# A transformer layer on one core: the second branch's projection moves from the merge into the attention

## The chip, the cores and the metric

The kernel runs on one core of a Trainium2 chip. The metric is the time of one execution in microseconds (us); a smaller one is better. Below, PE is the matrix engine (TensorE), DVE the vector engine, ACT the scalar engine, POOL the GpSimd engine, and SP the engine that here only issues transfers. Line numbers (L206) are those of the kernel's file.

## The reference

One layer of a diffusion backbone works on 256 latent tokens and 256 context tokens, 2048 wide. Cut to what matters here:

```
m_lat = split(silu(c) @ w_ada + b_ada, 6)       # modulation: six rows of 2048, the same for context
h  = rms_norm(x) * (1 + m_lat[1]) + m_lat[0]
p  = h @ w_in                                    # keys, values, queries and gates of both branches
oa = attention(rope(norm(qa)), ka_all, va_all)   # 16 heads of 128, 4 key heads
ob = diff_attention(rope(norm(qb)), kb_all, vb_all)   # 8 heads, two softmaxes subtracted, then a norm
merged = sigmoid(ga) * (oa @ w_br_a) + sigmoid(gb) * (ob @ w_br_b)
x1 = x + m_lat[2] * (merged @ w_out)
x2 = x1 + m_lat[5] * swiglu(rms_norm(x1) * (1 + m_lat[4]) + m_lat[3])
```

Here w_br_a is 2048x2048 and w_br_b 1024x2048. Only the latent tokens are carried on; context tokens give keys and values.

## The kernel before

Every large product is computed in three passes: an operand is split into a high part and the remainder (low part), and high x high (L210), high x low (L211) and low x high (L212) are summed in PSUM by `mm3`. Tokens stand in two tiles of 128 (`tk` 0 and 1). Weights come in pieces of 256 rows by 512 columns, 512 KB. `load_w` (L196) takes a piece by a transfer on SP's queue into a ring of 7 buffers (`wraw`), makes the high part on ACT (`whi`, L205) and the low part on DVE (`wlo`, L206), three buffers each. A piece is then 12 matmuls of 128x512 on PE: two row blocks, two token tiles, three passes. `project` (L534) is a generator: it loads pieces ahead, yields after each, and calls `tick()` (deferred work) and the function given as `side`. A result column group (`cg`) is 512 columns wide; its sums are handed to `evac`.

The stages around the change are these. After the context and the first half of the input projection come the attention's 32 units, 16 of branch b (the differential one) and 16 of branch a. A unit is cut into `front` (scores `s`, maximum on DVE L578, exponential on ACT L581) and `back` (transposes `ptp` L646, copies `pT` by ACT and DVE, product `o`). Between units the `filler` (L703) runs projection pieces so that PE has work while a softmax is under way: the query groups, whose evacuation is a long chain of norm and rotation (`norm_rope`, L393 to L416), and the eight gate projections, whose results ACT copies (L685) and POOL writes to DRAM (`gate_d`, L686). At unit 8 stands the keys stage: the keys of branch b's second half, then those and the values of branch a, with norms as well.

Two things run beside the filler's pieces, called by `side_work` (L692). `later` is the modulation: pieces of w_ada (`ada_pieces`, L353), each a 512 KB transfer and DVE instructions of 128x1024 that add a scaled row block to an accumulator (L364); its chunks 2, 4 and 3 are spread over the middle of the kernel, 96 such instructions. `chores` are the chains of the keys. Before, each call takes a chore, and every second call an ada as well.

The merge (from L736) goes over four column groups. For each, `load_gates` reads the stored gates of branch b back (POOL, L767) and takes their sigmoid (ACT, L768); w_br_b is projected in 4 pieces and its result multiplied by the gate (DVE, L775); then the same for w_br_a in 8 pieces, multiplied and added (L777, L778), and `turn` transposes the sum for the output projection. At the start the attention's results are split into high and low parts by `o_parts` (L216), and the last units' work is finished among the first pieces.

The order of the instructions on each engine is fixed when the program is built, by a list scheduler that follows the order of the code and priorities; `issue_after(x)` binds an instruction behind another. An engine works its list in that order, and an instruction that waits holds those behind it. The buffers that a transfer waits for are the ring's.

Of the kernel before, what the change touches and what calls it, by code (L numbers as in the profile page):

```python
# [11 lines left out]
F32 = mybir.dt.float32  # L12
# [23 lines left out]
WK = 2  # L36
# [10 lines left out]
def hybrid_block(ctx: ExitStack, tc: tile.TileContext, t: dict, out: bass.AP):  # L47
# [143 lines left out]
        nc.vector.tensor_scalar(out=neglam, in0=neglam, scalar1=-LAM_INIT, scalar2=None, op0=ALU.add)  # L191


    last_lo = []

    def load_w(src, r0, c0, nk=WK, in_big=False):  # L196
        raw = wp.tile([P, WK, CG], F32, tag="wraw", bufs=WRAW, name="wraw")
        nc.sync.dma_start(out=raw[:, 0:nk], in_=src[r0:r0 + nk * P, c0:c0 + CG].rearrange("(k p) c -> p k c", p=P))
        if in_big:
            both = big_tile("wbig", F32R).rearrange("p (h k c) -> p h k c", h=2, c=CG)  # L200
            hi, lo = both[:, 0], both[:, 1]
        else:
            hi = wp.tile([P, WK, CG], F32R, tag="whi", bufs=WHI, name="whi")
            lo = wp.tile([P, WK, CG], F32R, tag="wlo", bufs=WLO, name="wlo")
        nc.scalar.copy(out=hi[:, 0:nk], in_=raw[:, 0:nk])  # L205
# [472 lines left out]


    gate_d = dram.tile([2, 2, P, D], F32, name="gate_d")  # L680

    def gate_evac(w, cg):
        def f(tk, ps):
            g = scratch("gate")
            nc.scalar.copy(out=g, in_=ps)  # L685
            nc.gpsimd.dma_start(out=gate_d[w, tk, :, cg * CG:(cg + 1) * CG], in_=g)  # L686
        return f

    turns = [0]
    chores = [later_keys]  # L690
# [8 lines left out]
    gates = [(w, cg) for w in range(2) for cg in range(4)]  # L699
    units = [("b", u) for u in range(16)] + [("a", u) for u in range(16)]  # L700
    done, ready, started = set(), set(), []

    def filler():  # L703

        while len(started) < len(q_order) or gates:
            may = not gates or len(started) < 2 or a_done
            if may and len(started) < len(q_order) and len(started) - len(done) < 2:
                q = q_order[len(started)]
                started.append(q)
                for _ in q_group(*q):  # L710
                    pieces[0] += 1
                    yield None
                after(7, lambda q=q: ready.add(q))
            else:
                w, cg = gates.pop(0)
                for _ in project(w_in, xT, NKT, (GA0, GB0)[w] + cg * CG, gate_evac(w, cg), side=side_work):
                    pieces[0] += 1
                    yield None

    pieces = [0]  # L720
    all_pieces = (len(q_order) + len(gates)) * (NKT // WK)
    fill = filler()
    work = []

# [33 lines left out]
    w_bra, w_brb, w_out = t["w_br_a"][0], t["w_br_b"][0], t["w_out"][0]  # L758
    mT = Parts("mT", NKT)
    for cg in range(4):  # L760
        m = [scratch(f"m{tk}") for tk in range(2)]
        gs = {}

        def load_gates(w):
            for tk in range(2):
                g = scratch("gin", tag="p", bufs=4)
                nc.gpsimd.dma_start(out=g, in_=gate_d[w, tk, :, cg * CG:(cg + 1) * CG])  # L767
                nc.scalar.activation(out=g, in_=g, func=AF.Sigmoid)  # L768
                gs[w, tk] = g

        def gated(w):
            def f(tk, ps):
                g = gs[w, tk]
                if w == 1:
                    nc.vector.tensor_tensor(out=m[tk], in0=ps, in1=g, op=ALU.mult)  # L775
                else:
                    nc.vector.tensor_tensor(out=g, in0=ps, in1=g, op=ALU.mult)  # L777
                    nc.vector.tensor_tensor(out=m[tk], in0=m[tk], in1=g, op=ALU.add)  # L778
                    after(2 + tk, turn(tk))
            return f  # L780

        def turn(tk, cg=cg, m=m):
            def f():
# [4 lines left out]
                split(hi, lo, tp.rearrange("p (h q) -> p h q", h=4))  # L788
            return f

        if cg == 0:
            o_parts(4)
            o_parts(5)
        load_gates(1)
        for k, _ in enumerate(project(w_brb, oT, BH, cg * CG, gated(1), kt0=AH)):
            take(later, k % 2)
            if cg == 0:
                for w in list(work):
                    if next(w, w) is w:
                        work.remove(w)  # L800
                if k > 0:
                    o_parts(k - 1)
        if cg == 0:
            assert not work
            o_parts(3)
        load_gates(0)
        for k, _ in enumerate(project(w_bra, oT, AH, cg * CG, gated(0))):
            take(later, k % 2)
# [151 lines left out]
```

## Time and profile before

| | us |
|---|---|
| median of three runs | 1750.39 |
| lowest, highest | 1748.45, 1753.29 |
| profiled execution | 1752.44 |
| its span on the core | 1750.7 |
| PE busy in it | 1709.3 (98%) |
| DVE busy | 1128.9 (64%) |
| ACT busy | 773.2 (44%) |

The mean granted clock of PE in this execution is 0.993 of full speed. The profile counts as busy the time in which an engine has an instruction under way; matmuls overlap, so that one lasts 0.39 us while they follow each other every 0.22. Times in the trace count from the start of the span. In it, the keys stage lies at about 475 to 575, the passage from branch b to a at about 575 to 625, the units of a end at about 785, and the merge lasts to about 1000. The value PEclk of a window is the mean granted clock there; 1.00 is 2.4 GHz and 0.50 is 1.2 GHz.

### The profile page before, as it was taken

The page shows a single profiled execution, that of the slowest core. Times are in us where ns is not written, and L with a number is a line of the kernel's source. Part 1 is how long each engine was busy: PE and PEld are TensorE (multiplying, and loading weights), DVE is VectorE, ACT ScalarE, POOL GpSimd, SP SyncE. Part 2 cuts the span into 40 slices and gives each one's busy share as a digit, 9 for nine tenths or more (in the row PEclk, how much of TensorE's full clock was granted, in tenths as well). Part 3 has the DMA queues.
Part 4 walks back from the last instruction along what each step waited for, and adds up shares of the span by engine and source line. Part 5 has one row for each costly group of instructions (what it writes and reads, how often), then busy time and mean ns, then how long its engine had stood idle before and what let it go on. Part 6 is the DMA issues. An engine that isn't in the chain of part 4 may idle for free.

```text
span 1750.7 us, 21655 instructions
## 1 busy us (share of the span) xinstructions
PE 1709.3 (98%) x8106; PEld 1378.3 (79%) x8106; DVE 1128.9 (64%) x1416; ACT 773.2 (44%) x1061; POOL 126.5 (7%) x188
## 2 busy tenths in 40 slices
PE   5999999999999999999999999999999999999998
PEld 3767778887877788878888878888888888888887
DVE  4754658888798786968556664555566555454554
ACT  4422223246655566575444454444444444333332
POOL 2100001001132200001000100000000000000000
PEclk8999999999999999999999999999999999999999
DMA  9867785687776665648786756677777777666662
GB/s 271 281 222 262 239 306 181 195 269 246 223 231 222 204 236 175 212 133 278 245 288 225 251 176 190 203 239 233 238 239 239 234 237 232 208 197 214 219 204 90
DMA packets 190600, 393.47 MB, mean 225 GB/s; under 512 B 13120, under 2 KB 25488, under 8 KB 189984
## 3 DMA queue, kind: packets, MB, share of 16 engines
q1 hardware_dynamic: 183824, 369.71, 65.2%
q0 software_dynamic: 6672, 22.39, 4.1%
q8 instruction: 63, 1.03, 0.2%
q14 instruction: 41, 0.34, 0.1%
HBM read 383.62 MB, written 8.42 MB: 224 GB/s over the span
## 4 chain that ended last, share of the span: by engine, by line
PE 88%; DVE 5%; issue 3%; DMA 2%; ACT 1%; POOL 1%; SPq 1%; ACTq 0%; DVEq 0%; POOLq 0%
PE mm L211 27%; PE mm L210 26%; PE mm L212 26%; PE ada L266 2%; DVE wlo L206 1%; DMA wraw<-in_w_in_dram 1%; PE ptp L646 1%; PE s L626 1%; PE o L664 1%; ACT whi L205 1%; PE ftp L902 1%; DVE ada L364 0%; PE o L211 0%; DMA wada<-in_w_ada_dram 0%; PE o L210 0%
## 5 line engine op out<-in xcount | busy, mean ns | idle before, releaser
L206 DVE TENSOR_TENSOR wlo<-wraw,whi 128x1024 fp32r<-128x1024 f32 (+1 forms) x506 | 611.0, 1210 | 472.0 <-ACT whi L205 471.6
L205 ACT CAST whi<-wraw 128x1024 fp32r<-128x1024 f32 (+1 forms) x506 | 527.2, 1043 | 800.1 <-PE mm L212 685.4
L211 PE MATMUL mm<-wlo,hT 128*128 128x512 f32 x696 | 271.0, 389 | 2.0 <-DVE rstd L129 2.0
L210 PE MATMUL mm<-whi,hT 128*128 128x512 f32 x696 | 272.8, 392 | 0.0
L212 PE MATMUL mm<-whi,hT 128*128 128x512 f32 x696 | 271.2, 390 | 0.1
L210 PE MATMUL mm<-whi,xT 128*128 128x512 f32 x640 | 257.8, 407 | 2.3 <-ACT xT L215 1.8
L211 PE MATMUL mm<-wlo,xT 128*128 128x512 f32 x640 | 254.7, 398 | 4.9 <-DVE wlo L206 4.9
L212 PE MATMUL mm<-whi,xT 128*128 128x512 f32 x640 | 252.9, 395 | 0.0
L211 PEld LDWEIGHTS mm<-wlo,hT 128*128 128x128 f32 x696 | 130.7, 188 | 28.8 <-DVE wlo L206 2.4
L212 PEld LDWEIGHTS mm<-whi,hT 128*128 128x128 f32 x696 | 130.6, 188 | 27.7 <-DVE hT L216 0.5
L210 PEld LDWEIGHTS mm<-whi,xT 128*128 128x128 f32 x640 | 121.5, 190 | 39.3 <-issue 9.3
L364 DVE SCALAR_TENSOR_TENSOR ada<-wada,sc,ada 128x1024 f32<-128x1024 f32 x120 | 152.1, 1278 | 0.0
L210 PEld LDWEIGHTS mm<-whi,hT 128*128 128x128 f32 x696 | 130.7, 188 | 26.5
L211 PEld LDWEIGHTS mm<-wlo,xT 128*128 128x128 f32 x640 | 122.2, 191 | 30.5 <-DVE wlo L206 6.4
L212 PEld LDWEIGHTS mm<-whi,xT 128*128 128x128 f32 x640 | 122.0, 191 | 25.6
L210 PE MATMUL mm<-whi,fT 128*128 128x512 f32 x352 | 137.2, 390 | 0.0
L212 PE MATMUL mm<-whi,fT 128*128 128x512 f32 x352 | 137.0, 389 | 0.0
L211 PE MATMUL mm<-wlo,fT 128*128 128x512 f32 x352 | 136.9, 389 | 0.0
L210 PEld LDWEIGHTS mm<-whi,fT 128*128 128x128 f32 x352 | 66.1, 188 | 14.6 <-issue 0.8
L211 PEld LDWEIGHTS mm<-wlo,fT 128*128 128x128 f32 x352 | 66.1, 188 | 13.7
L212 PEld LDWEIGHTS mm<-whi,fT 128*128 128x128 f32 x352 | 66.1, 188 | 13.6
L210 PE MATMUL mm<-whi,cT 128*128 128x512 f32 x192 | 75.9, 395 | 0.4 <-ACT cT L215 0.4
(226 smaller groups left out, 2089.5 us busy)
## 6 DMA issues: line engine op xcount, KB each, us to landing
wada<-in_w_ada_dram SPq DMA_DIRECT2D x192, 512.0 KB, 4.5
wraw<-in_w_in_dram SPq DMA_DIRECT2D x154, 512.0 KB, 4.7
wraw<-in_w_ff_gate_dram SPq DMA_DIRECT2D x88, 512.0 KB, 4.2
wraw<-in_w_ff_up_dram SPq DMA_DIRECT2D x88, 512.0 KB, 4.1
wraw<-in_w_ff_down_dram SPq DMA_DIRECT2D x88, 512.0 KB, 4.8
wraw<-in_w_br_a_dram SPq DMA_DIRECT2D x32, 512.0 KB, 4.9
wraw<-in_w_out_dram SPq DMA_DIRECT2D x32, 512.0 KB, 5.2
wraw<-in_w_br_b_dram SPq DMA_DIRECT2D x16, 512.0 KB, 5.7
```

The source lines that it names most:

```text
L205: nc.scalar.copy(out=hi[:, 0:nk], in_=raw[:, 0:nk])
L206: last_lo.append(nc.vector.tensor_tensor(out=lo[:, 0:nk], in0=raw[:, 0:nk], in1=hi[:, 0:nk].bitcast(F32), op=ALU.subtract))
L210: nc.tensor.matmul(ps, lhsT=ah, rhs=wh, start=first, stop=False)
L211: nc.tensor.matmul(ps, lhsT=ah, rhs=wl, start=False, stop=False)
L212: nc.tensor.matmul(ps, lhsT=al, rhs=wh, start=False, stop=last)
L266: nc.tensor.matmul(aps[32 * g:32 * g + 32, 0:ncol], lhsT=cst[:, k, :], rhs=rhs, start=(k < 4), stop=(k >= NKT - 4))
L364: nc.vector.scalar_tensor_tensor(out=dst, in0=wt, scalar=sc[:, 0, kt:kt + 1], in1=dst, op0=ALU.mult, op1=ALU.add)
L626: nc.tensor.matmul(sps[i], lhsT=qT[rows, x, hh, tk * P:(tk + 1) * P], rhs=kT["b", grp][y][rows, hh, :], start=(n == 0), stop=(n == 2))
L646: nc.tensor.transpose(out=tp[:, kt * P:(kt + 1) * P], in_=p[:, kt * P:(kt + 1) * P], identity=ident)
L664: nc.tensor.matmul(op[:, 0:BV], lhsT=pT[:, kt, :], rhs=vb[:, kt, hh * BV:(hh + 1) * BV], start=(kt == 0), stop=(kt == 3))
L902: nc.tensor.transpose(out=tp[:, j * P:(j + 1) * P], in_=act[tk][:, j * P:(j + 1) * P], identity=ident)
```

## The change

The four column groups of w_br_b become the last entries of the filler's list, behind the eight gates: 16 pieces more between the units (128 instead of 112). As with the gates, ACT copies the sums and POOL writes them to DRAM, into a new tensor `prod_d`; one function, `to_dram`, serves both. The splits of branch b's output (`o_parts` 4 and 5) come just before, and those of branch a's first three quarters after units a6, a10 and a14.

`side_work` takes a chore first, and an ada only when there was no chore left and the keys stage of branch b is not running (`quiet`); then every second time, or two times of three once branch a has begun. The 96 ada of the chunks 2, 4 and 3 lay so before: 51 ahead of the keys stage, 9 in it, 28 among the a units and 8 in the merge. Now it is 53 ahead, none in the keys stage and 43 until the merge.

The merge keeps only w_br_a. `load_gated` is a generator of six steps for a column group, one per piece: reading a product back (L779), reading a gate (L783), its sigmoid (L786, bound behind the latest `whi`), and for branch b the product on DVE (L789, bound behind the latest `wlo`); then the gate of branch a.

```
-    def side_work():
-        turns[0] += 1
-        if turns[0] % 2:
-            take(later, 1)
-        take(chores[-1], 1)
+        if next(chores[-1], chores[-1]) is chores[-1] and not quiet:
+            turns[0] += 1
+            take(later, 1 if turns[0] % (3 if a_done else 2) else 0)
...
+    others += [(prod_d, oT, AH, t["w_br_b"][0], 0, cg) for cg in range(4)]
...
+                if kt0 and cg == 0:
+                    for g in (4, 5):
+                        o_parts(g)
+                for _ in project(w, src, BH if kt0 else NKT, c0 + cg * CG, to_dram(dst, cg), kt0=kt0, side=side_work):
...
+            quiet.append(True)
             for _ in keys("b", 1):
                 on()
                 take(fill, 2)
+            quiet.clear()
...
-    drain(fill)
+        if br == "a" and u % 4 == 2 and u > 4:
+            o_parts(u // 4 - 1)
+    for _ in fill:
+        on()
...
+        def load_gated():
             for tk in range(2):
+                m.append(scratch(f"m{tk}"))
+                nc.gpsimd.dma_start(out=m[tk], in_=prod_d[tk, :, cg * CG:(cg + 1) * CG])
+                yield None
+                for w in (1, 0):
+                    g = scratch("gin", tag="p", bufs=4)
+                    nc.gpsimd.dma_start(out=g, in_=gate_d[w, tk, :, cg * CG:(cg + 1) * CG])
+                    yield None
+                    with tc.issue_after(last_hi[-1].ins):
+                        nc.scalar.activation(out=g, in_=g, func=AF.Sigmoid)
+                    if w == 1:
+                        with tc.issue_after(last_lo[-1].ins):
+                            nc.vector.tensor_tensor(out=m[tk], in0=m[tk], in1=g, op=ALU.mult)
+                gs.append(g)
...
-        if cg == 0:
-            o_parts(4)
-            o_parts(5)
-        load_gates(1)
-        for k, _ in enumerate(project(w_brb, oT, BH, cg * CG, gated(1), kt0=AH)):
-            take(later, k % 2)
...
+        gates = load_gated()
+        for k, _ in enumerate(project(w_bra, oT, AH, cg * CG, gated)):
+            if k > 3:
+                take(later, 1)
+            if cg == 0 and k < 4:
+                on()
+                if k == 3:
+                    assert not work
+                    o_parts(3)
+            take(gates, 1)
```

How the order on the engines moves is shown at three places. The first is DVE in the keys stage of branch b; before, it reads (wlo is a weight's low part, nr, sq, ss and rstd belong to a norm of keys, kbT1 are keys turned, ada4 an accumulator of the modulation):

```order
L364 SCALAR_TENSOR_TENSOR ada4_2851<-wada2_4175,sc_107,ada4_2851 128x1024
L416 TENSOR_TENSOR nr_4184<-nr_4184,rstd_4181 128x512
L216 TENSOR_TENSOR kbT1_4040<-ktp_4190,kbT1_4039 128x4x128
L401 TENSOR_REDUCE ss_4238<-sq_4236 128x8
L410 TENSOR_TENSOR nr_4243<-kb1_118,rp_kb_1707 128x512
L129 TENSOR_SCALAR rstd_4240<-ss_4238 128x8
L412 TENSOR_TENSOR sq_4236<-kb1_118,rp_kb_1707 128x512
L206 TENSOR_TENSOR wlo_4262<-wraw_4259,whi_4261 128x1024
L414 TENSOR_TENSOR nr_4243<-nr_4243,sq_4236 128x8x32
L415 TENSOR_TENSOR nr_4243<-nr_4243,sq_4236 128x8x32
L206 TENSOR_TENSOR wlo_4280<-wraw_4277,whi_4279 128x1024
```

After the change the corresponding stretch, the norms of the same keys, reads:

```order
L206 TENSOR_TENSOR wlo_4317<-wraw_4314,whi_4316 128x1024
L416 TENSOR_TENSOR nr_4281<-nr_4281,rstd_4278 128x512
L216 TENSOR_TENSOR kbT1_4145<-ktp_4287,kbT1_4144 128x4x128
L129 TENSOR_SCALAR rstd_4336<-ss_4334 128x8
L410 TENSOR_TENSOR nr_4339<-kb1_118,rp_kb_1707 128x512
L412 TENSOR_TENSOR sq_4332<-kb1_118,rp_kb_1707 128x512
L206 TENSOR_TENSOR wlo_4358<-wraw_4355,whi_4357 128x1024
L414 TENSOR_TENSOR nr_4339<-nr_4339,sq_4332 128x8x32
L415 TENSOR_TENSOR nr_4339<-nr_4339,sq_4332 128x8x32
L206 TENSOR_TENSOR wlo_4376<-wraw_4373,whi_4375 128x1024
L416 TENSOR_TENSOR nr_4339<-nr_4339,rstd_4336 128x512
```

The row of ada4 (L364), which stood ahead of the end of a norm (L416) there and eight times more in the stage, is gone; the rows of wlo and of the norms alternate alone.

The second place is PE at the end of branch a's units. Before, the transposes of a unit's probabilities (ptp, four each) and the product that uses them (o from pT) stand one behind the other:

```order
L646 MATMUL ptp_7015<-ident_75,p_6947 128x128 x4
L646 MATMUL ptp_7022<-ident_75,p_6958 128x128 x4
L210 MATMUL o_7029<-pT_7014,vah_4611 128x256
L211 MATMUL o_7029<-pT_7014,vah_4611 128x256
L212 MATMUL o_7029<-pT_7014,val_4612 128x256
```

After, pieces of w_br_b (mm from oT4 and oT5, 12 matmuls each, of which one row stands here) lie between them:

```order
L646 MATMUL ptp_7312<-ident_75,p_7194 128x128 x4
L646 MATMUL ptp_7319<-ident_75,p_7205 128x128 x4
L210 MATMUL mm_7249<-whi_7328,oT4_6721 128x512
...
L210 MATMUL mm_7249<-whi_7349,oT5_6724 128x512
...
L210 MATMUL o_7365<-pT_7311,vah_4692 128x256
L211 MATMUL o_7365<-pT_7311,vah_4692 128x256
```

So two pieces come between the transposes and their product, where there was nothing.

The third place is POOL's list where the merge begins. Before, only reads of gates (gin, L767) stood there, of tensors written long ago. After, it reads (gate is here the copy of a product; adac_sb belongs to the modulation):

```order
L687 DMA prod_d_2817<-gate_7243 128x512
L687 DMA prod_d_2817<-gate_7246 128x512
L783 DMA gin_7485<-gate_d_2816 128x512
L783 DMA gin_7507<-gate_d_2816 128x512
L687 DMA prod_d_2817<-gate_7397 128x512
L372 DMA adac_sb_7404<-in_b_ada_dram 32x512
L687 DMA prod_d_2817<-gate_7400 128x512
L372 DMA adac_sb_7404<-in_b_ada_dram 32x512 x3
L779 DMA m0_7451<-prod_d_2817 128x512
L779 DMA m1_7531<-prod_d_2817 128x512
```

Two of the gates are read ahead of the last two writes of products; the first read of a product (m0) stands behind the last two writes and the biases.

One more place in words: on DVE the splits of oT4 and oT5 stood in the merge before. Now that of oT4, which the first piece of w_br_b needs, stands behind the norm of the last query group of branch a, ahead of that norm's last three rows; PE has there, between the group's last piece and that first one, the product of a unit and a unit's scores.

## Rows read from the trace of the kernel before

**Rows 1.** The page, part 1: engine, busy us, share of the span, instructions.

```profile
PE 1709.3 (98%) x8106; PEld 1378.3 (79%) x8106; DVE 1128.9 (64%) x1416; ACT 773.2 (44%) x1061; POOL 126.5 (7%) x188
```

**Rows 2.** Windows: from:to, length, busy us of each engine, PEclk, DMA share, GB/s.

```profile
475.00:550.00 75.00, 71.23 (x329) 55.31 (x328) 67.18 (x108) 42.83 (x73) 24.93 (x17) 0.95 0.69 217
...
575.00:625.00 50.00, 46.71 (x223) 37.67 (x222) 38.48 (x58) 22.28 (x40) 5.96 (x9) 0.97 0.68 218
625.00:750.00 125.00, 125.00 (x667) 106.55 (x666) 105.95 (x160) 82.47 (x146) 7.76 (x9) 1.00 0.59 200
750.00:800.00 50.00, 46.45 (x247) 38.36 (x246) 34.37 (x51) 38.13 (x69) 4.36 (x8) 0.97 0.40 127
800.00:1000.00 200.00, 199.96 (x900) 164.37 (x899) 125.78 (x130) 90.92 (x105) 18.19 (x34) 1.00 0.79 265
...
1025.00:1725.00 700.00, 700.00 (x3135) 578.79 (x3134) 379.00 (x343) 290.46 (x298) 8.60 (x16) 1.00 0.70 220
```

**Rows 3.** Windows, finer, around two of the stretches at the lower clock.

```profile
497.10:500.52 3.42, 3.42 (x9) 2.68 (x9) 1.89 (x4) 0.63 (x1) 2.72 (x1) 0.50 0.74 187
...
780.42:783.84 3.42, 3.42 (x14) 3.23 (x15) 2.30 (x2) 3.39 (x5) 0.00 (x0) 0.50 0.30 97
```

**Rows 4.** Waits of PE, 470 to 620, then 755 to 800: total us, times, longest.

```profile
PE mm L211 <- DVE wlo L206: 4.4, 3, 2.3
PE ptp L646 <- ACT junk_o L667: 1.3, 1, 1.3
PE s L626 <- ACT p L581: 1.2, 3, 0.7
...
PE o L210 <- DVE pT L216: 2.3, 2, 1.3
```

**Rows 5.** Lines of DVE, 486 to 548: instructions, busy us, mean ns, idle before.

```profile
L206 DVE TENSOR_TENSOR wlo<-wraw,whi 128x1024 fp32r<-128x1024 f32 x16 | 19.4, 1219 | 0.0
L364 DVE SCALAR_TENSOR_TENSOR ada<-wada,sc,ada 128x1024 f32<-128x1024 f32 x8 | 10.2, 1276 | 0.0
```

**Rows 6.** Timeline of PE, 492 to 498: start, length, then [idle before <-releaser].

```profile
496.58 0.50 PE L211 MATMUL mm<-wlo,xT 128*128 128x512 f32 x1 [2.29 <-DVE wlo L206]
```

**Rows 7.** Timeline of PE, 606 to 609.5, and of DVE, 598 to 612.

```profile
608.94 0.50 PE L211 MATMUL mm<-wlo,xT 128*128 128x512 f32 x1 [1.96 <-DVE wlo L206]
...
602.68 0.68 DVE L401 TENSOR_REDUCE ss<-sq 128x4 f32<-128x512 f32 x1
...
607.67 1.22 DVE L206 TENSOR_TENSOR wlo<-wraw,whi 128x1024 fp32r<-128x1024 f32 x1
```

**Rows 8.** Timeline of DVE, 695 to 708, and of PE, 702 to 708.

```profile
700.50 0.69 DVE L401 TENSOR_REDUCE ss<-sq 128x4 f32<-128x512 f32 x1 [1.14 <-ACT sq L399]
...
705.50 1.21 DVE L206 TENSOR_TENSOR wlo<-wraw,whi 128x1024 fp32r<-128x1024 f32 x1
...
706.93 0.39 PE L211 MATMUL mm<-wlo,xT 128*128 128x512 f32 x1
```

**Rows 9.** Timeline of PE, 776 to 783.

```profile
776.66 0.28 PE L211 MATMUL o<-pT,vah 128*128 128x256 f32 x1
776.78 0.29 PE L212 MATMUL o<-pT,val 128*128 128x256 f32 x1
...
779.76 0.36 PE L210 MATMUL o<-pT,vah 128*128 128x256 f32 x1 [1.26 <-DVE pT L216]
```

**Rows 10.** Lines of ACT, 800 to 1000.

```profile
L768 ACT ACTIVATE gin<-gin 128x512 f32<-128x512 f32 x12 | 7.6, 633 | 16.7 <-DMA gin<-gate_d 13.2 <-DVE ada L364 3.4
```

**Rows 11.** Source L686, then L767: issues of GpSimd (ns), and landing of their DMAs.

```profile
L686 POOL DMA_DIRECT2D gate_d<-gate x16: 539/584/633, 420.6 to 765.3; - x16
...
DMA to landing us min/median/max: 2.6/4.5/7.2
...
DMA to landing us min/median/max: 3.2/4.6/6.8
```

**Rows 12.** Windows: 612 to 796 as a whole.

```profile
612.00:796.00 184.00, 180.55 (x955) 152.72 (x954) 146.85 (x216) 124.87 (x219) 11.05 (x15) 0.99 0.56 189
```

More of the change, by code (lines that the diff above doesn't have):

```diff
@@ L204, in load_w @@
             lo = wp.tile([P, WK, CG], F32R, tag="wlo", bufs=WLO, name="wlo")
-        nc.scalar.copy(out=hi[:, 0:nk], in_=raw[:, 0:nk])
+        last_hi.append(nc.scalar.copy(out=hi[:, 0:nk], in_=raw[:, 0:nk]))
         last_lo.append(nc.vector.tensor_tensor(out=lo[:, 0:nk], in0=raw[:, 0:nk], in1=hi[:, 0:nk].bitcast(F32), op=ALU.subtract))
@@ L680, in hybrid_block, with to_dram @@
     gate_d = dram.tile([2, 2, P, D], F32, name="gate_d")
-    def gate_evac(w, cg):
+    prod_d = dram.tile([2, P, D], F32, name="prod_d")
+    def to_dram(dst, cg):
         def f(tk, ps):
@@ L685, in f @@
             nc.scalar.copy(out=g, in_=ps)
-            nc.gpsimd.dma_start(out=gate_d[w, tk, :, cg * CG:(cg + 1) * CG], in_=g)
+            nc.gpsimd.dma_start(out=dst[tk, :, cg * CG:(cg + 1) * CG], in_=g)
         return f
     turns = [0]
+    quiet = []
     chores = [later_keys]
     def side_work():
-        turns[0] += 1
-        if turns[0] % 2:
-            take(later, 1)
-        take(chores[-1], 1)
+        if next(chores[-1], chores[-1]) is chores[-1] and not quiet:
+            turns[0] += 1
+            take(later, 1 if turns[0] % (3 if a_done else 2) else 0)
     q_order = [("b", g) for g in range(2)] + [("a", g) for g in range(4)]
-    gates = [(w, cg) for w in range(2) for cg in range(4)]
+    others = [(gate_d[w], xT, 0, w_in, (GA0, GB0)[w], cg) for w in range(2) for cg in range(4)]
+    n_gates = len(others)
+    others += [(prod_d, oT, AH, t["w_br_b"][0], 0, cg) for cg in range(4)]
     units = [("b", u) for u in range(16)] + [("a", u) for u in range(16)]
@@ L703, in filler @@
     def filler():
-        while len(started) < len(q_order) or gates:
-            may = not gates or len(started) < 2 or a_done
+        while len(started) < len(q_order) or others:
+            may = not others or len(started) < 2 or a_done
             if may and len(started) < len(q_order) and len(started) - len(done) < 2:
@@ L754, in hybrid_block, with gated @@
         work.append(back(br, u, pr))
-    drain(fill)
-    w_bra, w_brb, w_out = t["w_br_a"][0], t["w_br_b"][0], t["w_out"][0]
+        if br == "a" and u % 4 == 2 and u > 4:
+            o_parts(u // 4 - 1)
+    for _ in fill:
+        on()
+    w_bra, w_out = t["w_br_a"][0], t["w_out"][0]
     mT = Parts("mT", NKT)
     for cg in range(4):
-        m = [scratch(f"m{tk}") for tk in range(2)]
-        gs = {}
-        def load_gates(w):
+        m, gs = [], []
+        def load_gated():
             for tk in range(2):
[L766 to L780, printed above, removed]
+                m.append(scratch(f"m{tk}"))
[11 more added lines that the diff above has]
+                gs.append(g)
+        def gated(tk, ps):
+            g = gs[tk]
+            nc.vector.tensor_tensor(out=g, in0=ps, in1=g, op=ALU.mult)
+            nc.vector.tensor_tensor(out=m[tk], in0=m[tk], in1=g, op=ALU.add)
+            after(2 + tk, turn(tk))
         def turn(tk, cg=cg, m=m):
@@ L789, in turn @@
             return f
-        if cg == 0:
-            o_parts(4)
-            o_parts(5)
-        load_gates(1)
-        for k, _ in enumerate(project(w_brb, oT, BH, cg * CG, gated(1), kt0=AH)):
-            take(later, k % 2)
[L797 to L808, printed above, removed]
+        gates = load_gated()
[8 more added lines that the diff above has]
+            take(gates, 1)
     drain(later)
```

7 lines of the change are left out of this document (3 added, 4 removed).

## The prediction

> **What bounds the kernel now.** I began with the engine line of the page. TensorE (PE) is busy 1709.3 of 1750.7 us, 98%; the vector engine (DVE) 64%, the scalar engine (ACT) 44% [rows 1]. PE's own work is the bound, and the order listing shows that the change leaves it alone: 7145 PE rows before, 7149 after. So only time that PE loses can be won: time in which it stands still, and time at the lower clock.
>
> Then I cut the part that the change touches into windows [rows 2]. From 625 to 750 us (first units of the softmax branch a), from 800 to 1000 (merge) and from 1025 to 1725 PE has no idle time to speak of, at a granted clock of 1.00. Three windows lose time: 475 to 550 us (71.23 busy of 75, clock 0.95), 575 to 625 (46.71 of 50, 0.97), 750 to 800 (46.45 of 50, 0.97). Standing still: 3.77 + 3.29 + 3.55 = 10.6 us. The clock: (1 - 0.95) x 75 + 0.03 x 50 + 0.03 x 50 = 6.75 us. In finer windows this is four stretches of 3.42 us at 0.50, the lower level (1.2 of 2.4 GHz), two of them in the first window (the first and the last of the four in [rows 3]); half of 4 x 3.42 is 6.8, the same sum. PE stood shortly before each of them, so a stall costs its length and then 1.7 us. All told 10.6 + 6.75 = 17.4 us. That is the ceiling of the gain.
>
> Third, the waits of these windows [rows 4]: matrix multiplications that wait for a weight's low part (wlo) on DVE, 4.4 us in three waits; scores and transposes that wait for ACT, 2.5; at the end of the attention the second product (o) for the transposed probabilities' low part (pT), 2.3.
>
> **The change part by part.** A matmul of 128x512 takes 700.00 / 3135 = 0.223 us [rows 2], so a piece of a projection (12) takes PE 2.7 us. On DVE it takes one wlo, 1.22, and a modulation piece (ada) another 1.28 [rows 5].
>
> (1) Keys stage, 475 to 550. PE stands 2.29 us for a wlo [rows 6]. In this stage DVE has 67.18 of 75 us of work [rows 2], in bursts, because the norms of the keys come on top of wlo and ada; in the listing nine ada lie in it, as in the piece shown with the change. Afterwards there are none: 9 x 1.28 = 11.5 us of DVE work leave, far more than the 3.77 that PE stood. The scores' waits for ACT I put to the same root, since the maximum that ACT needs first is made on DVE (L578), in the same queue. What is late next is a wlo behind a norm alone. I keep 1 us of loss; gain 3.77 + 3.75 - 1 = 6.5.
>
> (2) Passage from branch b to a, 575 to 625. The burst of the q norm, from the first sum (602.68) to the end of the wlo behind it (607.67 + 1.22), takes 6.2 us of DVE, and PE stood 1.96 us at 608.94 [rows 7]. The same burst at 700.50 to 706.71 cost nothing, PE going on at 706.93 [rows 8], since DVE came to it earlier. With chores ahead of ada the burst meets a shorter queue, but the chain is the same: I keep 1 us. Gain 3.29 + 1.5 - 1 = 3.8.
>
> (3) End of the attention, 750 to 800. Before, the last units stand nearly bare: transposes and the product that uses them follow one another (the fence of the change), and PE stood 1.26 us at 779.76 for pT, then fell to half clock [rows 9]. The change brings 16 more pieces of filler (43 us of PE work, taken out of a merge that was full), two of them, 5.4 us, between a unit's transposes and its product. That covers the wait. Gain 3.55 + 1.5 = 5.05.
>
> (4) A new hand-over. The filler's first piece with oT4 comes after the last q group. PE has from that group's end 12 matmuls of 0.12 us (776.66 to 776.78 in [rows 9]), 6 of 0.223 and 8 more until the first that needs the low part of oT4: about 4.6 us. DVE does the norm of q first, 5.0 us from the first sum to what stands behind it [rows 8], begun some 0.5 us before the group's end, since half of its results is complete 1.3 us ahead and ACT squares it in between; then the split of oT4, 128x1024 as a wlo, 1.2 us: ready at 5.7 us. So 1.1 us of stall; if an ada and a wlo ahead of it are still running it is 1.28 + 1.22 more, 3.6, and then 1.7 for the clock, 5.3. If DVE is ahead, as at 700, it is 0. I take 1.1, the nearer to [rows 8].
>
> (5) Round trip of the products. ACT copies each of the 8 results (0.63, by ACT's sigmoid of 128x512 [rows 10]), GpSimd (POOL) writes it to DRAM and reads it back. The reads stand in POOL's queue behind the last write's landing; ACT's sigmoids and DVE's new product L789 stand in front of casts and wlo. For the first group: the first half of the last product leaves PE 1.3 us before T0 (the end of that piece); + 0.63 copy + 0.58 issue + 4.5 landing = T0 + 4.4; read 0.58 + 4.6 = T0 + 9.6 [rows 11]. By the order PE has 10.7 us of pieces, one unit's product and eight transposes, and wants the wlo behind L789 at T0 + 13.9; less 1.22 and 0.7 L789 must start by T0 + 12.0. Slack 2.4. With the slowest landings of the rows, 7.2 and 6.8, it misses by 2.5, and costs 4.2 with the clock. In the three later groups a read issued 2.0 us after the group before ended is followed by the sigmoid and a cast that PE wants 11.7 us after; slack about 2.3. I take 0, for the median landings; the range holds 4.2. A gain is excluded, since PE loses nothing there today.
>
> (6) DVE among the a units. Its work there was 146.85 of 184 us [rows 12], and now has 16 wlo more, some 15 ada that came from the keys and the merge, and 5 splits fewer: 146.85 + 19.5 + 19.2 - 6.1 = 179 plus what the filler brings on the half units, at most 192, over 184 + 43 - 8 = 219 us. That is 82 to 88%. The window 625 to 750 had 85% without a loss [rows 2], so nothing is charged, at 0 to 4 bursts like the one at 606. The weights' DMA: two ada loads for three pieces are 5 x 0.52 MB in 3 x 2.7 + unit work, some 11.5 us, 228 GB/s; the merge ran at 265 [rows 2]. Nothing.
>
> (7) Merge: out go w_br_b's pieces and 8 ada. It was at 199.96 of 200, so this saves nothing there.
>
> Sum: 6.5 + 3.8 + 5.05 - 1.1 = 14.3 us. The profiled execution took 1752.44, so 1738.1; from the median of the runs, 1750.39, 1736.1. I give 1737.
>
> A rule that speaks against (5): by the Trainium skill, page "SBUF — State Buffer", section "A bandwidth-pool intuition that's wrong (but worth ruling out)", a transfer that GpSimd issues and that takes about 620 ns alone takes about 3100 ns under a DVE copy, as its descriptors cannot be written. The trace does not show it: with DVE 85% busy the gate writes issue in 539 to 633 ns and land in 2.6 to 7.2 us [rows 11]. Nothing in the sum rests on it; were it so for the new products, the first rival below would be its form.
>
> **The rivals.**
>
> Slower: the round trip holds the weights. Its place is L789 and the sigmoids in front of wlo and cast in the merge, which today loses nothing. For it: the chain write, landing, read is new, and today's writes have their landing hidden by hundreds of us. Against: the median landings leave 2.3 us. Price: if landings were doubled (9.0 and 9.2), the first group would be 9.1 - 2.4 = 6.7 late + 1.7 clock, the three later ones 4.6 - 2.3 + 1.7 = 4.0 each: 20.4 against the gain of 14.3, that is 6 us slower, about 1757. It begins beyond a landing of 6.9 us and decides at about 8.5.
>
> Smaller: the hand-over (4) costs its upper end, 5.3, and the keys keep half of their stall (2.3 more): 14.3 - 4.2 - 2.3 = 7.8, 1743. For it: DVE is denser there than at 700. Against: the splits of oT0 to oT2 come between the units.
>
> Same: DVE is the hidden bound of the denser a units, and each of the four a bursts stalls as that at 606 did, 2.0 + 1.7 us. Then 4 x 3.7 = 14.8, which takes the gain away: 1750. For it: three of four places now have ada twice in three turns. Against: [rows 8].
>
> **How the numbers follow.** The forecast 0.60, with its own range 1732 to 1741; the smaller gain 0.16; the same 0.13; slower 0.11. A measurement of this kernel tells some 0.3% from no change, 5.25 us, so faster is below 1745.1 and slower above 1755.6: faster 0.60 + 0.16 = 0.76, same 0.13, slower 0.11. The low end is the ceiling with a little for the clock: 1750.39 - 17.4 = 1733, and 4 us below that for what the windows round, 1729. The high end takes in the case without gain: 1751.
>
> **What would show it.** In the changed kernel's windows: the keys stage without waits for wlo above 1 us and a clock of at least 0.98 (1); one wait or none behind the first a norm (2); no wait of o for pT at the end of the attention (3); a wait for oT or wlo of about 1 us, not 4, at the first oT4 piece (4); landings of prod_d and of the reads at 4 to 5 us, and the merge still full (5); DVE below 90% among the a units without waits of PE for wlo (6). I am wrong if the merge shows idle time on PE, if DVE reaches 95% among the a units, or if as many half-clock stretches as before stand elsewhere.

## The result, and the profile after

The changed kernel takes 1738.31 us (median of four runs, 1737.21 to 1742.26) against 1751.09 of the kernel before on the same chip: ratio 0.993, 95% interval 0.9917 to 0.9943, some 12.8 us faster. A second series, beside the variants below, gave 1736.51 against 1750.64, ratio 0.9931 (0.9918 to 0.9945). The forecast was 1737, within 1729 to 1751. The profiled execution took 1737.67 us, its span is 1735.9, its mean clock 0.998. One run of 2141.18 us of the kernel before and one of 6071.88 us of a variant are left out of the medians below.

The first line of its page, beside [rows 1]:

```profile
PE 1701.6 (98%) x8106; PEld 1372.9 (79%) x8106; DVE 1128.3 (65%) x1416; ACT 776.9 (45%) x1069; POOL 135.9 (8%) x204
```

PE does as many matmuls as before (8106). Of the 14.8 us by which the span is shorter, PE is busy 7.7 us less with the same work, which is put down to the clock (the forecast had 6.75), and stands 7.1 us less (the forecast, 10.6 less what it left, 7.5).

The windows of the changed kernel's trace, with the bounds and columns of [rows 2]:

```profile
475.00:550.00 75.00, 74.28 (x370) 59.65 (x369) 63.86 (x108) 47.54 (x82) 19.21 (x18) 1.00 0.62 190
...
575.00:625.00 50.00, 49.06 (x247) 37.94 (x247) 42.06 (x69) 29.49 (x56) 13.01 (x17) 1.00 0.74 238
625.00:750.00 125.00, 123.71 (x642) 104.19 (x641) 108.42 (x156) 79.41 (x132) 8.80 (x10) 1.00 0.68 225
750.00:800.00 50.00, 50.00 (x270) 42.85 (x269) 42.52 (x57) 36.46 (x65) 3.30 (x6) 1.00 0.76 253
800.00:1000.00 200.00, 198.56 (x919) 163.30 (x917) 127.46 (x147) 100.76 (x130) 29.55 (x55) 1.00 0.77 256
```

What is to be seen: the keys stage lost 3.77 us of standing and 3.75 of clock and now loses 0.72 and nothing; the passage 3.29 and 1.5, now 0.94 and nothing; 750 to 800, which held the end of the units, is full. New are 1.29 us between 625 and 750 and 1.44 behind 800; of the latter 0.50 are a wait for pT, the rest belongs to the stall at the end of the merge, which lay behind 1000 before. No window from 400 to 1725 us has a clock below 1.00.

What PE waited for between 400 and 1010 us (total us, times, longest), beside [rows 4]:

```profile
PE mm L211 <- DVE wlo L206: 2.6, 2, 2.0
PE mm L212 <- DVE oT L216: 1.3, 1, 1.3
PE s L626 <- ACT p L581: 0.8, 2, 0.5
PE o L664 <- DVE kaT L216: 0.7, 1, 0.7
PE o L211 <- DVE pT L216: 0.5, 1, 0.5
```

The waits of the product for pT are down from 2.3 to 0.5, and those for a low part from 4.4 to 2.6. Of these 2.6, 2.0 are one wait at the end of the merge, in front of the FFN, which the kernel before had in the same size, for another instruction of DVE (rstd, L129). The 1.3 for oT is the new hand-over.

### The profile page after: what moved, and what is told of

It is laid out like the page before. It is cut to its first block, busy times and chain, and to the rows that moved or that the text cites. A ratio compares the mean times of both kernels' runs of the same rounds, so it can differ in the third digit from the quotient of the medians.

```text
span 1735.9 us, 21726 instructions
## 1 busy us (share of the span) xinstructions
PE 1701.6 (98%) x8106; PEld 1372.9 (79%) x8106; DVE 1128.3 (65%) x1416; ACT 776.9 (45%) x1069; POOL 135.9 (8%) x204
## 4 chain that ended last, share of the span: by engine, by line
PE 68%; DVE 4%; issue 3%; ACT 1%; POOL 1%; DMA 0%; DVEq 0%; POOLq 0%; ACTq 0%
PE mm L212 21%; PE mm L211 21%; PE mm L210 21%; PE ptp L646 1%; DVE wlo L206 1%; PE o L664 1%; PE ftp L910 1%; PE s L626 1%; PE o L211 0%; PE o L212 0%; PE o L210 0%; PE s L210 0%; PE s L212 0%; PE s L211 0%; DVE nr L416 0%
## 5 line engine op out<-in xcount | busy, mean ns | idle before, releaser
L364 DVE SCALAR_TENSOR_TENSOR ada<-wada,sc,ada 128x1024 f32<-128x1024 f32 x120 | 152.0, 1277 | 0.3 <-DVE rs L582 0.3
L212 PEld LDWEIGHTS mm<-whi,fT 128*128 128x128 f32 x352 | 66.1, 188 | 13.9
```

The lines of the kernel that those rows point to most:

```text
L212: nc.tensor.matmul(ps, lhsT=al, rhs=wh, start=False, stop=last)
L364: nc.vector.scalar_tensor_tensor(out=dst, in0=wt, scalar=sc[:, 0, kt:kt + 1], in1=dst, op0=ALU.mult, op1=ALU.add)
```

## The experiments

Each kernel was timed against the kernel before on its own chip, so the ratios are what is compared, and a gain is the difference of the two medians on one chip. In the profiled executions the part ahead of the change scatters: the same modulation row (L381) starts at 347.1 to 351.1 us in them, and differences of 2 us between two spans can lie there. Where a place is judged it is by windows and waits.

**The two halves of the change.** First the new order of the side work alone, put into the kernel before:

```
+        if next(chores[-1], chores[-1]) is chores[-1] and not quiet:
+            turns[0] += 1
+            take(later, 1 if turns[0] % (3 if a_done else 2) else 0)
...
+            quiet.append(True)
             for _ in keys("b", 1):
```

> The kernel before with only the new order of the side work: chores first, modulation pieces only when no chore is left, none in the keys stage of branch b; the merge, its w_br_b pieces and the loading of the gates stay as they were. Theory (the loss of the keys stage and of the passage from b to a comes from modulation pieces between the norms on the vector engine): both terms come, 6.5 + 3.8 us, and the end of the attention still loses its 5; so 10 us faster than before, about 1741, with no wait for a weight's low part above 1 us and a granted clock of at least 0.98 between 475 and 575 us, and 3 to 5 us of waits and clock at the end of the units. Rival (the pieces of filler are what brings the time, the order of the side work little): within 4 us of before, 1747 to 1751.

1739.63 against 1752.29, ratio 0.9931 (0.9917 to 0.9945): as much as the whole change, as far as this can be measured. Its windows:

```profile
475.00:550.00 75.00, 74.89 (x377) 60.38 (x376) 65.31 (x111) 48.54 (x87) 21.73 (x18) 1.00 0.61 189
...
575.00:625.00 50.00, 49.52 (x241) 39.09 (x240) 45.38 (x75) 27.46 (x49) 7.33 (x8) 1.00 0.77 254
...
750.00:830.00 80.00, 76.52 (x376) 62.07 (x375) 58.21 (x70) 50.79 (x79) 9.12 (x17) 0.98 0.68 222
```

The keys stage and the passage stand 0.11 and 0.48 us; the last row is the end of the units without the filler, 3.48 us of standing and a clock of 0.98, as before. The theory's numbers hold: the gain is 2 us larger than was put, of which 1.4 are seen in the two windows, where nearly nothing is left. Whether the pieces between the norms are the cause is asked further below.

Then the other half, the changed kernel with the old order of the side work:

```
-        if next(chores[-1], chores[-1]) is chores[-1] and not quiet:
...
+        turns[0] += 1
+        if turns[0] % 2:
+            take(later, 1)
+        take(chores[-1], 1)
```

> The changed kernel with the old order of the side work: every call takes a chore and every second one a modulation piece, the keys stage included (6 of them lie in it); w_br_b stays filler of the attention and the merge stays changed. Theory (terms are separate): the end of the attention gains 5, the hand-over costs 1.3, the keys stage and the passage lose as before; 3.8 us faster than before, about 1747, with the waits for low parts at about 494 and 607 us and half-clock stretches behind them back. Rival (where the modulation lies does not matter as long as the filler is longer): 1738, as the changed kernel.

1743.97, ratio 0.9958 (0.9944 to 0.9972): 8.3 us faster than before, 4.5 more than was expected. Its windows:

```profile
475.00:550.00 75.00, 72.34 (x349) 57.00 (x348) 68.13 (x110) 45.35 (x78) 22.56 (x16) 1.00 0.70 224
550.00:575.00 25.00, 23.26 (x119) 17.50 (x118) 17.85 (x27) 11.98 (x21) 7.24 (x12) 1.00 0.94 299
575.00:625.00 50.00, 47.34 (x235) 37.56 (x234) 42.81 (x72) 28.60 (x56) 7.20 (x7) 0.97 0.62 194
```

Keys stage and passage lose again (2.66 and 2.66 us), and 1.74 us between them: there the scores wait for adac_sb on DVE (L382), which itself stood 3.03 us for a transfer of biases. But the clock in the keys stage is 1.00 where it was 0.95, and that is what the expectation had not allowed. The two halves are worth 12.7 and 8.3 us alone and 12.8 to 14.1 together; they don't add: with the filler alone the keys stage already stands less and at full clock, so that the side work finds less there to take.

**Which rule of the side work.** The rule for the keys stage alone, in the kernel before:

```
-        if turns[0] % 2:
+        if turns[0] % 2 and not quiet:
             take(later, 1)
...
+            quiet.append(True)
             for _ in keys("b", 1):
...
+            quiet.clear()
```

> The kernel before with only the rule that keeps modulation pieces out of the stage in which branch b's second keys are normalized; elsewhere every call still takes a chore and every second one a modulation piece, so three lie in the keys of branch a and the rest as before. Theory (the rule is worth what stood in its stage): the wait at 494 to 497 us and the half clock behind it go, 2.3 + 1.7, about 1748; the waits of the scores at 525 to 530 and of the weight at 607 stay. Rival (the rule is worth nothing, as taking it out of the changed kernel cost nothing): 1752.

1740.12, ratio 0.9950 (0.9938 to 0.9963), a larger gain than the 1748 expected:

```profile
475.00:550.00 75.00, 73.75 (x372) 59.29 (x371) 68.56 (x114) 48.34 (x85) 20.11 (x18) 1.00 0.69 215
...
575.00:625.00 50.00, 49.40 (x246) 39.71 (x247) 43.12 (x72) 28.01 (x50) 6.35 (x8) 1.00 0.69 224
```

And chores first alone, in the kernel before, the first diff of `side_work` without the lines that set and clear `quiet`:

> The kernel before with only chores first (modulation only in calls that find no chore left), without the rule for the keys stage. Theory (that order brings nearly all of what the new order of the side work brought, 12.7 us): 1740 to 1742, no wait above 1 us between 475 and 625 us. Rival (both rules share it): about 1746, with the wait at 494 to 497 us still there.

1744.32, ratio 0.9968 (0.9959 to 0.9977):

```profile
475.00:550.00 75.00, 71.46 (x339) 56.35 (x338) 65.51 (x107) 43.50 (x73) 23.00 (x18) 0.95 0.65 203
...
575.00:625.00 50.00, 49.12 (x244) 38.85 (x244) 43.44 (x65) 26.51 (x47) 5.31 (x7) 1.00 0.77 256
```

Of the two the first row differs. Without the rule the keys stage stands 3.54 us at a clock of 0.95, with the same 2.3 us for a low part as before; with it 1.25 us at 1.00. The passage clears under either, 0.60 and 0.88 us left. So both expectations were half right: in these traces the rule takes most of the stall of the keys and chores first doesn't, but either of them takes that of the passage. The trace of chores first is of a run of 1749.15 us, where the other ten took 1742.31 to 1745.92, so a typical run may lose less there than it shows.

The rule in the changed kernel, the other way round:

```
-            quiet.append(True)
...
-            quiet.clear()
```

> The changed kernel without the one rule that keeps modulation pieces out of the keys stage of branch b; chores still come first. By the order three modulation pieces lie between the norms of these keys, where the changed kernel has none. Theory (a modulation piece between two norms makes a weight's low part late): one stall of 1.5 to 2.5 us and a half-clock stretch behind it return there, 3 to 4 us slower than the changed kernel, about 1742. Rival (chores first is what counts, the three pieces find room): 1738, no wait above 0.7 us there.

1737.19, ratio 0.9917 (0.9902 to 0.9932): not slower. The theory falls for this kernel. Its keys stage:

```profile
475.00:550.00 75.00, 74.23 (x369) 59.59 (x368) 68.47 (x112) 47.97 (x81) 20.76 (x16) 1.00 0.70 220
```

DVE does 68.47 us of work here, more than the 67.18 of before [rows 2], and PE stands 0.77 us instead of 3.77. In it are six modulation instructions (L364) where before had ten, and 22 low parts for 19, since PE comes further in the same 75 us. So a DVE that is 91% busy doesn't by itself make PE stand. That what stands in front of one low part when PE needs it is what counts, and that the longer filler (four pieces per unit for three and a half) shifts it, is argued, not shown.

**The hand-over.** The splits of oT4 and oT5 given out earlier:

```
-                if kt0 and cg == 0:
-                    for g in (4, 5):
-                        o_parts(g)
...
+        if br == "a" and u in (3, 5):
+            o_parts(4 + u // 4)
```

> The changed kernel with the splits of branch b's output (oT4 and oT5) given out after units a3 and a5 instead of right before the first piece of w_br_b. It tests the hand-over: in the changed kernel TensorE waits 1.29 us at 747.79 us for the low part of oT4, which stands behind the norm of the last queries. Theory: that wait goes and none above 0.5 us takes its place, 1.3 us less: 1737, at the edge of what can be measured, so it is read from the trace. Rival (what waits there is the norm's burst, whoever stands behind it): TensorE waits about as long for a weight's low part near the same place.

1734.60, ratio 0.9900 (0.9886 to 0.9914), the fastest of all; the interval lies just below those of the changed kernel's two series. Its windows:

```profile
625.00:750.00 125.00, 125.00 (x650) 106.00 (x650) 110.57 (x161) 81.91 (x138) 7.88 (x9) 1.00 0.68 221
750.00:830.00 80.00, 80.00 (x424) 67.23 (x423) 58.32 (x73) 54.48 (x88) 11.91 (x22) 1.00 0.80 264
```

The 1.29 us are gone and nothing takes their place; the gain is 17.4 us, against 12.8 and 14.1 of the two series, so 3 to 5 us more where this wait gives 1.3. Where the rest comes from isn't settled. With the rule for the keys taken out as well:

> The changed kernel with both: no rule that keeps modulation pieces out of the keys stage of branch b (alone that measured 1737.2, not slower), and the early splits of oT4 and oT5. If both wait places are as read, the attention keeps a wait of about 0.7 us in the keys stage and 1 us at the passage, none at the hand-over: 1736, 1 to 3 us faster than the changed kernel. If the early splits meet the modulation pieces in a new place: 1738 or more, with a wait for a low part between 600 and 700 us.

1737.00 (median of four runs), ratio 0.9915 (0.9901 to 0.9929): not clearly told apart from the changed kernel or from the early splits alone, though its trace has no wait at the hand-over either. It has the two waits for low parts (1.4 us together, in the keys stage and at the passage) that taking out the rule alone has. The waits are those that the first theory named; its 1736 is within the scatter, and the second's new place isn't there.

**The round trip.** The last products by a longer way:

```
+            nc.gpsimd.dma_start(out=hop_d[0][tk] if late else dst[tk, :, cg * CG:(cg + 1) * CG], in_=g)
+            if late and tk == 1:
...
+                        nc.gpsimd.dma_start(out=to, in_=hop_d[h][i])
```

> The changed kernel in which the products of the last column group go through two more tensors in DRAM (two more copies by GpSimd) before the merge reads the group; what is computed is the same, though the values read are those of the last group only for that group. It tests the slower rival of the prediction, the round trip that holds the weights. In the changed kernel the first product on the vector engine waits 0.6 us for its read and starts at 821.16 us, and the low part behind it is ready 4.1 us before TensorE takes it. In this kernel the order puts that product one low part later, so 6.8 us are free. The two copies delay the read by about 2 x (0.54 + 4.6) = 10.3 us. Theory (the product holds the low parts behind it on its engine): TensorE stands about 3.5 us for a low part in the first group of the merge, with or without 1.7 us of clock, so 3.5 to 5 us slower than the changed kernel, 1742 to 1743. Rival (the read is hidden, or what stands behind it can go on): no wait there, 1738.

1738.49, ratio 0.9925 (0.9910 to 0.9939): no difference, but not a test of the theory. GpSimd's timeline:

```profile
818.45 0.54 POOL L694 DMA_DIRECT2D prod_d<-hop_d  x1 [1.13 <-DMA hop_d<-hop_d]
818.99 0.57 POOL L786 DMA_DIRECT2D m<-prod_d  x1
```

The read m follows the last copy by its issue time, without waiting for its landing. It reads the first column group, and the copies are of the last; the first products are written from 762 us on, more than 50 us before the read. So the chain of the prediction (last write, landing, read) isn't one of data. The read waits in the changed kernel all the same, as its row below shows; for what (a buffer of the ring that the copy `gate` shares with `m`, or a count of transfers under way) no run told apart. A chain that is real:

```
+                if cg == 0 and tk == 0:
+                    for h in hop_d:
+                        with tc.issue_after(stored[-1].ins):
+                            stored.append(nc.gpsimd.dma_start(out=h, in_=src))
+                        src = h
+                nc.gpsimd.dma_start(out=m[tk], in_=src)
...
+        with tc.issue_after(((hold.pop(0) if hold else None) or last_hi[-1]).ins):
```

> The changed kernel in which the first product of the merge's first group is read by way of three copies in DRAM, one behind the other, begun after the last write of products; the order of the vector engine is bound so that the product still stands in front of the same low part (the fourth of the group). The longer way in the run before had not delayed that read: it had only 3 us of effect, as a copy lands in about 3 us and the read did not depend on it, and the product stood one low part later. Here the chain is real: three copies of 3.1 to 3.6 us each put the product from 821 to about 831 us. Theory (the slower rival's mechanism holds, but the place has 4.1 us of slack): TensorE stands about 6 us for that low part, then perhaps 1.7 us of clock; 6 to 8 us slower than the changed kernel, 1744 to 1746. Rival (the place is covered in some other way): 1738 and no wait above 1 us in the first group.

1745.79, ratio 0.9962 (0.9949 to 0.9974): a gain of 6.2 us for 12.8 and 14.1, so 6.6 to 7.9 us slower than the changed kernel (5.5 by the ratios), about as the theory said. In its timeline the product on DVE, the low part behind it, and PE (in this kernel L797 is the product and L207 the low part):

```profile
832.68 0.69 DVE L797 TENSOR_TENSOR m<-m,gin 128x512 f32<-128x512 f32 x1 [6.79 <-DMA m<-hop_d]
833.29 2.35 DVE L207 TENSOR_TENSOR wlo<-wraw,whi 128x1024 fp32r<-128x1024 f32 x2
...
834.56 0.80 PE L212 MATMUL mm<-wlo,oT 128*128 128x512 f32 x1 [6.19 <-DVE wlo L207]
```

and the windows behind the wait:

```profile
834.00:838.00 4.00, 3.44 (x8) 2.77 (x9) 3.38 (x4) 0.00 (x0) 0.97 (x2) 0.50 0.66 203
...
830.00:850.00 20.00, 15.44 (x58) 12.54 (x59) 11.29 (x13) 4.74 (x5) 2.90 (x7) 0.83 0.69 220
```

The product waits 6.79 us for its read, PE 6.19 for the low part, and then runs at 0.50; the clock of 0.83 over 20 us makes 3.4 us, of which some 0.8 fall into the wait itself (0.80 from 830 to 834): more than the 1.7 that was expected. Beside it, the same place in the changed kernel (POOL, DVE, PE):

```profile
816.05 0.57 POOL L779 DMA_DIRECT2D m<-prod_d  x1 [1.30 <-DMA prod_d<-gate]
...
821.16 0.69 DVE L789 TENSOR_TENSOR m<-m,gin 128x512 f32<-128x512 f32 x1 [0.57 <-DMA m<-prod_d]
821.77 1.22 DVE L206 TENSOR_TENSOR wlo<-wraw,whi 128x1024 fp32r<-128x1024 f32 x1
...
827.09 0.39 PE L211 MATMUL mm<-wlo,oT 128*128 128x512 f32 x1
```

The low part is ready at 822.99 and PE takes it at 827.09: 4.1 us free. The product came 10.2 us later in the variant (11.5 by the two timelines, of which 1.3 lie in the part ahead), and 10.2 - 4.1 = 6.1. The mechanism of the slower rival is real; its place had 4.1 us of slack and none was used.

**One step a piece.** All loads, sigmoids and products of a group at its start:

```
-                yield None
...
-                    with tc.issue_after(last_hi[-1].ins):
-                        nc.scalar.activation(out=g, in_=g, func=AF.Sigmoid)
+                    nc.scalar.activation(out=g, in_=g, func=AF.Sigmoid)
```

> The changed kernel whose merge gives out the two products, the four gates, their sigmoids and the products on the vector engine of a column group all at its beginning, instead of one step per piece bound behind a cast or a low part. Theory A (the steps matter: sigmoids that wait for a landing of 4 to 6 us stand in front of the casts on the scalar engine): each of the four groups makes TensorE wait once, 1 to 3 us, with a half-clock stretch behind some; 5 to 12 us slower than the changed kernel, 1743 to 1750. Theory B (the three buffers of high and low parts cover it, as before the change, where the sigmoids waited 13.2 us for their reads and TensorE never): no wait in the merge, 1738.

1744.87, ratio 0.9960 (0.9947 to 0.9973): a gain of 7.2 us for 12.8 and 14.1, so 5.6 to 6.9 us slower than the changed kernel (5 by the ratios). What PE, ACT and DVE waited for in its merge:

```profile
PE o L211 <- DVE pT L216: 1.8, 1, 1.8
PE mm L211 <- DVE wlo L206: 1.5, 5, 0.4
...
ACT gin L783 <- DMA gin<-gate_d: 24.3, 9, 5.0
...
DVE m L785 <- DMA m<-prod_d: 16.2, 5, 4.9
```

ACT stands 24.3 us for gates that it reads ahead of casts, DVE 16.2 for products; PE's share is 1.8 us for pT and five short waits of 0.3 us on average. The steps matter, as theory A said, but not in its form: PE lost 3.3 us in waits, 1.8 of them in one, and no clock. The span of the profiled execution is 6.9 us longer than the changed kernel's; 2.0 of the rest lie ahead of 351 us, where the code is the same, and 1.6 are not placed.

## Why the prediction was right, point by point

The method first: loss as standing time plus (1 - clock) x length in the windows of the touched part, 17.4 us before; the stall of 2.0 us at the end of the merge, which all kernels have, is left out. The last columns are the gain by this loss, the gain in the same profiled executions, read from the first to the last modulation row (L381; 1155.3 us before), and the gain measured as difference of medians.

| kernel | loss, us | gain by loss | same executions | measured |
|---|---|---|---|---|
| changed | 0.72 + 0.94 + 1.29 + 0.50 = 3.5 | 13.9 | 15.3 | 12.8 |
| changed, second series | 0.72 + 0.93 + 1.29 = 2.9 | 14.5 | 15.9 | 14.1 |
| side work alone | 0.11 + 0.48 + 3.48 + 1.6 = 5.7 | 11.7 | 13.2 | 12.7 |
| filler alone | 2.66 + 1.74 + 2.66 + 1.5 + 1.43 = 10.0 | 7.4 | 6.9 | 8.3 |
| rule for the keys alone | 1.25 + 0.60 + 3.56 + 1.6 + 0.7 = 7.7 | 9.7 | 11.6 | 10.5 |
| chores first alone | 3.54 + 3.75 + 0.88 + 3.56 + 1.2 = 12.9 | 4.5 | 4.0 | 6.3 |
| without the rule for the keys | 0.77 + 0.83 + 1.29 + 0.16 = 3.0 | 14.4 | 14.6 | 15.1 |
| early split | 0.71 + 0.92 + 0 = 1.6 | 15.8 | 17.9 | 17.4 |
| early split, without the rule | 0.73 + 0.85 = 1.6 | 15.8 | 16.7 | 15.0 |
| longer way of the last products | 0.70 + 0.93 + 1.29 = 2.9 | 14.5 | 16.0 | 13.8 |
| late first product | 0.71 + 0.93 + 1.30 + 1.76 + 4.56 + 3.2 = 12.5 | 4.9 | 7.1 | 6.2 |
| loads at once | 0.71 + 0.92 + 1.30 + 1.81 + 1.57 = 6.3 | 11.1 | 10.4 | 7.2 |

Within the same executions all agree within 2.2 us, and all but the last agree with the medians within 2 us. The early split gains the whole ceiling of 17.4 us with 1.6 still lost, so the ceiling, too, holds only to 2 us. So where the time was lost, and how much of it could be won, the prediction had right. Two things it did not have. The cause that it gave for its largest term, the keys stage, is not shown. And the clock term, 6.75 of the 17.4 us, belongs to one execution: the mean clock of the kernel before lies between 0.993 and 0.998 in the runs on record, and the profiled one, 0.993, is the lowest. A typical run may lose less to the clock, so that the sum meets the medians this closely is in part luck.

Keys stage (1): 1 us was left in the forecast, 0.72 came, without clock; right in size, but by luck: the forecast left a low part behind a norm, and what came is one wait of a product o (L664) for DVE, with no wait for a low part. That the stage won because 11.5 us of DVE work left it is not shown: DVE's busy time in the window fell only from 67.18 to 63.86 us, and the variant without the rule has 68.47 and hardly stands. What holds is that the rule by itself, in the kernel before, takes the stage's standing from 3.77 to 1.25 us.

Passage (2): 1 us forecast, 0.94 came. Chores ahead of modulation were given as the cause; the rule for the keys alone did the same, so it is only one way to get there; how the norm's burst comes to miss PE is not shown.

End of the units (3): forecast 0, came 0.50 for pT, in one of the two traces of the changed kernel. The variants without the filler all keep the loss of about 3.5 us there: the filler takes it, as was argued.

Hand-over (4): forecast 1.1, came 1.29, and no clock behind it, as was taken. The rows from the changed kernel's timeline (DVE, PE):

```profile
741.53 0.28 PE L210 MATMUL o<-pT,vah 128*128 128x256 f32 x1
...
741.53 0.68 DVE L401 TENSOR_REDUCE ss<-sq 128x4 f32<-128x512 f32 x1
...
745.93 0.68 DVE L412 TENSOR_TENSOR sq<-mm,rp_qa 128x512 f32<-128x512 f32 x1
746.53 1.21 DVE L216 TENSOR_TENSOR oT<-o,oT 128x1024 fp32r<-128x1024 f32 x1
...
747.79 0.50 PE L212 MATMUL mm<-whi,oT 128*128 128x512 f32 x1 [1.29 <-DVE oT L216]
```

The group's last piece ends where o begins, at 741.53. The norm runs without a gap from there, 5.0 us to the split at 746.53, and PE takes oT at 747.79, when it is done. That is the mechanism of the prediction, and the early split removed it. Two of its sizes were off and nearly cancel: the norm began at the group's end and not 0.5 us before it, behind a low part, and PE had 4.97 us of work to that point (to 746.50) and not 4.6, as transposes lie among it.

Round trip (5): no cost, as forecast; but its working put the slack at 2.4 us where it is 4.1, and took the write's landing for the start of a data chain that the longer way showed not to be one. Price and mechanism of the rival, beyond that slack, came as worked out (6.19 us for 6.1). The landing of 6.9 us at which the prediction lets this rival begin is that of its three later groups; by its own slack of 2.4 the first group would have been late from 5.8 on. The landings:

```profile
L687 POOL DMA_DIRECT2D prod_d<-gate x8: 539/542/602, 762.1 to 812.7; - x8
...
DMA to landing us min/median/max: 3.1/4.8/6.7
...
DMA to landing us min/median/max: 3.7/5.7/6.8
```

Writes land in 4.8 us in the median (4.5 before, [rows 11]), reads of products in 5.7, and the writes' issues take 539 to 602 ns with DVE at 85% (750 to 800 us). The Trainium skill (page "SBUF — State Buffer", section "A bandwidth-pool intuition that's wrong (but worth ruling out)") gives some 3100 ns for a GpSimd transfer under a DVE copy. The prediction set this against its own case, but this trace does not try it: among DVE's instructions between 760 and 814 us are differences, scaled sums, maxima and reciprocals, and no copy.

DVE among the a units (6): 82 to 88% forecast for 219 us; from 612 to 831 us it was busy 177.47, 81%, and 87% in the densest window, 625 to 750 (108.42 of 125). Of PE's waits for it there only the hand-over and the 0.50 for pT came. Merge (7): 160.00 of 160 us busy from 830 to 990, as full as before, no gain, as said; what the prediction did not say is that the new loads would have cost there if they weren't spread over the pieces.

The rival of a smaller gain needed the hand-over's upper end, the one of no change stalls at four bursts; neither is in the trace.

## What to carry to other kernels

When one engine is at 98%, add up its standing time and its lost clock window by window: that sum bounds what a reordering there can win, and what is left of it in a variant's trace tells the gain to about 2 us. Take the clock's part of it as one execution's. A load on a second engine need not cost by its sum in the stage (68.47 of 75 us cost 0.77 here); what the late first product cost was set by the slack of the one low part behind it; two changes of order that each clear the same stall don't add. Work moved out of a full stage must bring its loads back one at a time, with the slack of each known: here 4.1 us, read from the timeline and borne out by a product that came 10.2 us later.

## What the runs showed that was not expected

The price of the clock behind a stall isn't fixed. In the kernel before, four stalls were followed by 3.42 us at 0.50; in the changed kernel PE stood 1.29 us at the hand-over and 2.0 at the end of the merge, and the granted clock stayed 1.00; in the filler alone the keys stage stood 2.66 us at 1.00, with chores first alone 3.54 us at 0.95. The clearest case is the end of the units, where the kernel before and the one with chores first alone stand equally long:

```profile
750.00:830.00 80.00, 76.45 (x383) 63.22 (x382) 57.45 (x74) 52.68 (x86) 7.42 (x14) 0.98 0.60 201
...
750.00:830.00 80.00, 76.44 (x389) 62.05 (x388) 53.61 (x67) 51.63 (x80) 9.12 (x17) 1.00 0.58 189
```

The first row is before, at 0.98; the second, with the same 2.3 us for pT, stays at 1.00. At the end of the merge it is the other way round: behind the same 2.0 us the clock from 1000 to 1025 us is 1.00 before and 0.93 with chores first alone. It isn't fixed for a kernel either: the eleven runs of chores first alone have mean clocks from 0.995 to 1.000. What decides it was not tried.

Copies of 256 KB from DRAM to DRAM, issued by GpSimd, landed in 2.8 to 5.4 us on the longer way (four, median 4.2) and in 2.8 to 6.4 for the late first product (three, median 3.1), so in no more time than the writes from SBUF (3.1 to 6.7, median 4.8).
